# Casting and splitting the next weights ahead of, instead of behind, the background tasks of their slot

## The chip, the cores and the metric

The kernel runs on one core of a Trainium2 chip. The metric is the time of one execution on the device in microseconds (us), as the median of several runs; a profile of one further execution comes with it.

## What is computed

The reference passes one sequence of 256 tokens of width 2048 through three blocks, in float32. Cut to the products and what hangs on them:

```python
# block 1
proj = rms_norm(x) @ w_in                      # 2048 x 12288, split in ten
y_r  = rwkv7(p_r, p_k, p_v, ...) * silu(z_r)   # a recurrence over 256 tokens, 16 heads of 64
y_a  = band_attention(q, k, v) * silu(z_a)
merged = sigmoid(m_r) * (y_r @ w_branch_rwkv) + sigmoid(m_a) * (y_a @ w_branch_attn)
x = x + rms_norm(merged @ w_out)
# block 2
proj = rms_norm(x) @ w_in_2                    # queries, keys, index scores, gates
attn = top-k sparse attention;  sgu = spatial gating unit
x = x + (sigmoid(ga) * attn + sigmoid(gb) * sgu) @ w_out_2
x = x + relu(rms_norm(x) @ w_ff1) ** 2 @ w_ff2        # 2048 x 8192 x 2048
# block 3
x = rms_norm(x);  y = [pool_mixer, dilated attention] of rms_norm(x) @ w_in_3
x = x + [rms_norm(y_pool), rms_norm(y_attn)] @ w_out_3
x = x + relu(rms_norm(x) @ w_up) ** 2 @ w_down
out = rms_norm(x)
```

Most of the work is in some 580 MB of weights, each of which is read once and multiplied by 256 columns of activations.

## The kernel before

**Panels and groups.** Every weight matrix is cut into panels of 512 output columns (`Panel`, two are narrower). A panel's rows are taken in groups: one group is 512 rows by 512 columns, loaded as two halves (weight units) of 128 x 1024 floats, 512 KB each. A panel of a 2048-row matrix has four groups, one of a 1024-row matrix (the two branch matrices and the output matrix of block 3) has two. `Builder.run` (L187) walks over all groups of all panels in order. In a group it works through four output tiles, j = 0 to 3 (the code calls them units; I call one with what is issued after it a **slot**, and a weight unit always a half). Slot j issues 8 matmuls for each pair, 4 rows of tiles times 2: L250 multiplies the rounded weights `whi` by a 512-wide operand, which holds the rounded activations and their remainder, and L251 the weights' remainder `wlo` by the 256 rounded activations. All add up in the PSUM tile `pm` of tag m0 to m3; each tag has one buffer, so the next panel's tile j can be begun when this panel's has been read out. Panels in mode "T" swap the operands (L256 to L258) and have two slots.

**Weight units.** `cut(i, u)` (L202 to L213) makes half u of group i ready: ScalarE casts it (L210, `whi`), VectorE subtracts (L211, `wlo`). `whi` and `wlo` have four buffers each, which is two groups: the cast of half 0 of group i+1 can begin when the last matmuls of group i-1 that read half 0 are done, which is in that group's slot 3. While group i is multiplied, `cut(i + 1, 0)` is issued in slot 0 and `cut(i + 1, 1)` in slot 1. In mode T half 0 is cut ahead of the slots, and half 1 in slot 0.

**Evacuations.** When the last group of a panel has issued tile j, the panel's evacuation is started (`start`, L180, called in L261). Most begin with `sum_halves` (L270): ScalarE copies the right half of `pm` to `ev` (L273; L617, L697 and L1111 are the same copy in other panels), and a step later VectorE adds the left half (L276). So the copy waits for TensorE to finish that very tile. What follows differs by panel: gates, products, and the split of a result into `mg`, `hid` or `yah` (L281 on ScalarE, L283 on VectorE), which are operands of later panels.

**Background tasks.** Attention, the RWKV recurrence (`rwkv`, L729; its inner part `gram`, L917), top-k, the pooling mixer and the norms are Python generators. Each issues a few instructions on TensorE, VectorE, ScalarE, GpSimd or a DMA, then yields n, and is taken up again n steps later. They have no queue of their own: their instructions stand in the same in-order engine queues as the weights' and the matmuls'. The numbers of the yields are set by hand, so that a result is there by the time TensorE comes to the instruction that reads it.

**The order in a slot.** `step` (L132) first moves the evacuations on by a piece each, then each background task. Ahead of the change, a slot ends so:

```python
                self.step(j in when)          # evacuations, then background tasks
                if last:
                    self.start(p.evac(j, out))
                if j in when:
                    cut(i + 1, when.index(j))
```

`when` is (0, 1) for four slots. `busy` (true in a slot with a cut) holds older evacuations back for that slot, and some tasks (the axpy steps of the recurrence, L867 to L874, and top-k) skip it.

Of the kernel before, what the change touches and what calls it, by code (L numbers as in the profile page):

```python
# [66 lines left out]
class Builder:  # L67
# [62 lines left out]
        self.bgs.append([gen, 0])  # L130

    def step(self, busy=False):  # L132

        self.busy = busy
        lazy = 0 if busy else 3
        for e in list(self.evq):
            if e[1] and not lazy:
                continue
            lazy -= e[1]
            e[1] = 1  # L140
            if next(e[0], True):
                self.evq.remove(e)
        for b in list(self.bgs):
            if b[1] > 0:
                b[1] -= 1
                continue
            try:
                n = next(b[0])
                b[1] = (n or 1) - 1
            except StopIteration:  # L150
                self.bgs.remove(b)
# [29 lines left out]
    def run(self, panels):  # L181
        groups = [(p, g) for p in panels for g in range(p.ngroups)]
        n = len(groups)
        raw, split = {}, {}
        loaded = [0]

        def load(upto):  # L187
            while loaded[0] < min(upto, 2 * n):
                u = loaded[0]
                p, g = groups[u // 2]  # L190
                t = self.stage.tile([128, p.half, p.ncols], F32, name="wf", tag="wf", bufs=5)
                raw[u] = t
                k = g * p.kg + (u % 2) * p.half
                if p.load:
                    p.load(t, k)
                else:
                    src = p.w[p.c0 // p.ncols, (p.k0 + k) // p.half]
                    self.nc.sync.dma_start(t, src.rearrange("p (k c) -> p k c", c=p.ncols))
                self.after.pop(u, lambda: None)()
                loaded[0] += 1  # L200

        def cut(i, u):  # L202
            if i >= n:
                return
            p, g = groups[i]
            hs, ls = split.setdefault(i, ([], []))
            t = raw.pop(2 * i + u)
            hi = self.stage.tile([128, p.half, p.ncols], F32R, name="whi", tag="whi", bufs=4)
            lo = self.stage.tile([128, p.half, p.ncols], F32R, name="wlo", tag="wlo", bufs=4)
            self.nc.scalar.copy(hi, t)  # L210
            self.nc.vector.tensor_tensor(lo, t, hi.bitcast(F32), op=ALU.subtract)  # L211
            hs.append(hi)
            ls.append(lo)  # L213

        load(5)
        cut(0, 0)
        cut(0, 1)
        ps = {}
        nt = 1
        mm = self.nc.tensor.matmul  # L220
        for i, (p, g) in enumerate(groups):
            if g == 0 and p.pre:
                p.pre()
            load(2 * i + 7)
            hs, ls = split.pop(i)
            if g == 0:
                nt = (nt + 1) % 2 if p.mode == "T" else 1
                ps = {}
            last = g == p.ngroups - 1
            if p.mode == "F":  # L230
                units = [(j, f"m{j}") for j in range(p.ncols // 128)]
            else:
                units = [(j, f"m{2 * nt + j}") for j in range(2)]

            when = (0, 1) if len(units) == 4 else (-1, 0 if len(units) == 2 else -1)
            for u in range(2):
                if when[u] < 0:
                    cut(i + 1, u)
            for j, tag in units:
                if g == 0:  # L240
                    ps[j] = self.pm.tile([128, 512], F32, name="pm", tag=tag)
                out = ps[j]
                for kk in range(p.kg):
                    hi, lo = hs[kk // p.half][:, kk % p.half, :], ls[kk // p.half][:, kk % p.half, :]
                    a = p.act(g * p.kg + kk)
                    st = g == 0 and kk == 0
                    en = last and kk == p.kg - 1
                    if p.mode == "F":
                        c = slice(j * 128, (j + 1) * 128)
                        mm(out, hi[:, c], a, start=st, stop=False, skip_group_check=True)  # L250
                        mm(out[:, 256:512], lo[:, c], a[:, 0:256], start=False, stop=en, skip_group_check=True)  # L251
                    else:
                        ah = a[:, j * 128:(j + 1) * 128]
                        al = a[:, 256 + j * 128:256 + (j + 1) * 128]
                        o = out[:, :p.ncols]
                        mm(o, ah, hi, start=st, stop=False, skip_group_check=True)  # L256
                        mm(o, ah, lo, start=False, stop=False, skip_group_check=True)  # L257
                        mm(o, al, hi, start=False, stop=en, skip_group_check=True)  # L258
                self.step(j in when)
                if last:  # L260
                    self.start(p.evac(j, out))  # L261
                if j in when:
                    cut(i + 1, when.index(j))
                if p.mode == "T":
                    self.step()
            if last and p.post:
                p.post()
# [1484 lines left out]
```

## Time and profile before

| | |
|---|---|
| median of 3 runs | 3312.41 us (3309.85 to 3313.7) |
| profiled execution, its time | 3309.79 us |
| its span | 3307.9 us |
| TensorE matmul busy | 3238.6 us (98% of the span) |
| VectorE busy | 2076.2 us (63%) |
| ScalarE busy | 1710.5 us (52%) |
| GpSimd busy | 560.0 us (17%) |
| moved by DMA | 589.88 MB, mean 178 GB/s |

Some 1.9 us lie between the span and the execution's own time. Busy shares are means over very different stages: from 1300 to 2300 us and from 2600 to 3280 us two feed-forward blocks run nearly alone, while the recurrence runs beside the projections from about 350 to 720 us, and three attentions and the other tasks elsewhere. A mean of 98% on TensorE leaves 69.3 us of the span in which no matmul is shown, and these lie in a few stages.

### The profile page before, as it was taken

What the parts mean: (1) busy time and instruction counts of PE and PEld (TensorE: products, weight loads), DVE (VectorE), ACT (ScalarE), POOL (GpSimd) and SP (SyncE); (2) the same over time, 40 slices, a digit from 0 to 9 for tenths busy, and PEclk for the clock granted to TensorE, in tenths of its full rate; (3) what the DMA queues carried; (4) which work ended last, traced back from release to release, by engine and by line L of the source; (5) the groups of instructions that cost most, each with busy time, mean ns of one, the idle gap of its engine ahead of it and who ended that gap; (6) DMA issues with size and microseconds to landing.
All of it is one profiled execution on the core that took longest, in us unless ns stands there. A gap on an engine that the chain in (4) does not pass through costs nothing.

```text
span 3307.9 us, 50068 instructions
## 1 busy us (share of the span) xinstructions
PE 3238.6 (98%) x19182; PEld 2797.5 (85%) x19182; DVE 2076.2 (63%) x3058; ACT 1710.5 (52%) x2868; POOL 560.0 (17%) x570
## 2 busy tenths in 40 slices
PE   8999999999999999999999999999999999999998
PEld 7887778888778888888888888888888888888887
DVE  5677677666567556676565555557757665555556
ACT  5555444455443654455545455555455655545454
POOL 2232031214310421243000000003215200000001
PEclk9999999999899999999999999999999999999999
DMA  6544545456445555656655565556555565566554
GB/s 206 185 160 159 152 124 172 151 161 203 152 149 187 177 166 177 198 181 191 192 191 185 187 198 189 186 191 195 175 172 166 185 191 188 187 198 189 183 189 147
DMA packets 175583, 589.88 MB, mean 178 GB/s; under 512 B 28784, under 2 KB 31984, under 8 KB 175344
## 3 DMA queue, kind: packets, MB, share of 16 engines
q1 hardware_dynamic: 174624, 585.47, 55.8%
q8 instruction: 150, 2.46, 0.3%
q10 hardware_dynamic: 720, 1.22, 0.1%
q14 instruction: 89, 0.73, 0.1%
HBM read 582.95 MB, written 3.67 MB: 177 GB/s over the span
## 4 chain that ended last, share of the span: by engine, by line
PE 86%; DVE 6%; issue 3%; ACT 3%; POOL 1%; DMA 0%; DVEq 0%; POOLq 0%; ACTq 0%
PE pm L250 51%; PE pm L251 26%; DVE wlo L211 3%; PE pm L256 2%; PE pm L258 2%; PE pm L257 2%; ACT whi L210 2%; PE psc L341 1%; DVE ev L276 0%; PE ppv L375 0%; PE ptr L368 0%; POOL ev L671 0%; PE pst L302 0%; PE ppl L1622 0%; DMA b<-bias 0%
## 5 line engine op out<-in xcount | busy, mean ns | idle before, releaser
L211 DVE TENSOR_TENSOR wlo<-wf,whi 128x1024 fp32r<-128x1024 f32 x1086 | 1351.5, 1268 | 1091.8 <-ACT whi L210 1081.9
L250 PE MATMUL pm<-h,whi 128*128 128x512 f32 x3872 | 1377.0, 398 | 11.1 <-ACT whi L210 7.8
L210 ACT CAST whi<-wf 128x1024 fp32r<-128x1024 f32 x1086 | 1106.2, 1050 | 463.8 <-PE pm L250 374.2
L251 PE MATMUL pm<-h,wlo 128*128 128x256 f32 x3872 | 1091.4, 282 | 16.1 <-DVE wlo L211 15.6
L250 PEld LDWEIGHTS pm<-h,whi 128*128 128x128 f32 x3872 | 729.6, 188 | 181.5 <-ACT whi L210 8.2
L251 PEld LDWEIGHTS pm<-h,wlo 128*128 128x128 f32 x3872 | 735.4, 190 | 24.9 <-DVE wlo L211 24.2
L250 PE MATMUL pm<-hid,whi 128*128 128x512 f32 x2048 | 711.2, 391 | 0.0
L251 PE MATMUL pm<-hid,wlo 128*128 128x256 f32 x2048 | 573.5, 280 | 0.0
L273 ACT COPY ev<-pm 128x256 f32<-128x256 f32 x491 | 180.7, 368 | 702.9 <-PE pm L251 687.1
L250 PEld LDWEIGHTS pm<-hid,whi 128*128 128x128 f32 x2048 | 383.1, 187 | 84.8
L250 PE MATMUL pm<-hb,whi 128*128 128x512 f32 x1168 | 419.3, 401 | 12.1 <-DVE hb L727 9.2
L251 PEld LDWEIGHTS pm<-hid,wlo 128*128 128x128 f32 x2048 | 387.1, 189 | 0.0
L1103 POOL TENSOR_TENSOR acc<-acc,sqa 128x256 f32<-128x256 f32 x104 | 117.1, 1131 | 1497.7 <-ACT sqa L1098 1474.1
L251 PE MATMUL pm<-hb,wlo 128*128 128x256 f32 x1168 | 329.6, 282 | 1.4 <-DVE wlo L211 1.1
L250 PEld LDWEIGHTS pm<-hb,whi 128*128 128x128 f32 x1168 | 220.9, 189 | 68.2 <-issue 9.5
L251 PEld LDWEIGHTS pm<-hb,wlo 128*128 128x128 f32 x1168 | 223.0, 191 | 4.1 <-DVE wlo L211 2.9
L276 DVE TENSOR_TENSOR ev<-pm,ev 128x256 f32<-128x256 f32 x491 | 199.1, 417 | 25.5 <-ACT ev L273 25.1
L250 PE MATMUL pm<-mg,whi 128*128 128x512 f32 x512 | 178.0, 391 | 0.0
L251 PE MATMUL pm<-mg,wlo 128*128 128x256 f32 x512 | 143.7, 281 | 0.9 <-DVE wlo L211 0.9
L250 PEld LDWEIGHTS pm<-mg,whi 128*128 128x128 f32 x512 | 95.8, 187 | 21.2 <-DVE ev L276 0.2
L251 PEld LDWEIGHTS pm<-mg,wlo 128*128 128x128 f32 x512 | 96.8, 189 | 1.9 <-DVE wlo L211 1.9
L256 PE MATMUL pm<-whi,hb 128*128 128x512 f32 x160 | 66.0, 412 | 0.0
(350 smaller groups left out, 3004.5 us busy)
## 6 DMA issues: line engine op xcount, KB each, us to landing
wf<-w_in SPq DMA_DIRECT2D x312, 512.0 KB, 4.0
wf<-w_ff SPq DMA_DIRECT2D x256, 512.0 KB, 4.4
wf<-w_sgu SPq DMA_DIRECT2D x128, 512.0 KB, 3.9
wf<-w_up SPq DMA_DIRECT2D x128, 512.0 KB, 4.3
wf<-w_down SPq DMA_DIRECT2D x128, 512.0 KB, 4.4
wf<-w_out SPq DMA_DIRECT2D x96, 512.0 KB, 4.3
wf<-w_branch_attn SPq DMA_DIRECT2D x16, 512.0 KB, 3.6
wf<-w_branch_rwkv SPq DMA_DIRECT2D x16, 512.0 KB, 4.3
```

Source lines behind the costliest of these rows:

```text
L210: self.nc.scalar.copy(hi, t)
L211: self.nc.vector.tensor_tensor(lo, t, hi.bitcast(F32), op=ALU.subtract)
L250: mm(out, hi[:, c], a, start=st, stop=False, skip_group_check=True)
L251: mm(out[:, 256:512], lo[:, c], a[:, 0:256], start=False, stop=en, skip_group_check=True)
L256: mm(o, ah, hi, start=st, stop=False, skip_group_check=True)
L257: mm(o, ah, lo, start=False, stop=False, skip_group_check=True)
L258: mm(o, al, hi, start=False, stop=en, skip_group_check=True)
L273: nc.scalar.copy(a, p[:, 256:512])
L276: nc.vector.tensor_tensor(b, p[:, 0:256], a, op=ALU.add)
L341: nc.tensor.matmul(p[:, a:2 * a + 128], qa[:, a:a + 128], ka[:, 0:a + 128], start=True, stop=True)
L1103: nc.gpsimd.tensor_tensor(accs[0], accs[0], s, op=ALU.add)
```

## The change

`step` is divided in two: `evacs`, which moves the evacuations, and `tasks`, which moves the background tasks. In a slot with a weight unit, the unit is now cut between the two, and so also ahead of the start of the slot's own evacuation.

```diff
     def step(self, busy=False):
+        self.evacs(busy)
+        self.tasks()
+
+    def evacs(self, busy=False):
 
         self.busy = busy
         lazy = 0 if busy else 3
@@ -140,6 +144,9 @@
             e[1] = 1
             if next(e[0], True):
                 self.evq.remove(e)
+
+    def tasks(self):
+
         for b in list(self.bgs):
             if b[1] > 0:
                 b[1] -= 1
@@ -256,11 +263,12 @@
                         mm(o, ah, hi, start=st, stop=False, skip_group_check=True)
                         mm(o, ah, lo, start=False, stop=False, skip_group_check=True)
                         mm(o, al, hi, start=False, stop=en, skip_group_check=True)
-                self.step(j in when)
+                self.evacs(j in when)
+                if j in when:
+                    cut(i + 1, when.index(j))
+                self.tasks()
                 if last:
                     self.start(p.evac(j, out))
-                if j in when:
-                    cut(i + 1, when.index(j))
                 if p.mode == "T":
                     self.step()
```

The set of instructions is the same on every engine, and with line numbers left out the order on TensorE, GpSimd and SyncE (which issues the loads) is too. On ScalarE 365 of the 1086 casts stand further ahead, on VectorE 104 of the 1086 subtractions; the lines of the changed file are 7 or 8 higher (cast L217, subtraction L218, `ev` copy L281).

The first place is ScalarE at the end of the last panel ahead of those of `w_branch_rwkv` and in the first of those (about 750 us): `ev<-pm` are the copies of slots 0, 1, ..., the casts between them make the next group ready, and `mg` are splits of the branch's result. Before:

```order
L273 COPY ev<-pm 128x256
L210 CAST whi<-wf 128x1024
L273 COPY ev<-pm 128x256
L210 CAST whi<-wf 128x1024
L281 CAST mg<-ev_7650 128x256
L273 COPY ev<-pm 128x256
```

Now:

```order
L217 CAST whi<-wf 128x1024
L281 COPY ev<-pm 128x256
L217 CAST whi<-wf 128x1024
L281 COPY ev<-pm 128x256
L289 CAST mg<-ev_7650 128x256
L281 COPY ev<-pm 128x256
```

Each cast stands ahead of the copy of its own slot instead of behind it. 267 of the 365 moved casts pass such a copy, 240 of them nothing else. VectorE's order at this place is the same as before.

The second place is VectorE in the recurrence (about 390 us, at the end of a panel): `S`, `P`, `gs` and `yc` are results of background tasks, `ev` are evacuations. Before:

```order
L1008 TENSOR_TENSOR S<-pY,DC 128x256
L211 TENSOR_TENSOR wlo<-wf,whi 128x1024
L276 TENSOR_TENSOR ev_3934<-pm,ev 128x256
L559 TENSOR_TENSOR ev_3934<-ev_3934,rb 128x256
L929 TENSOR_TENSOR P<-pgr,mask_90 128x512 x2
L1037 TENSOR_REDUCE gs<-pY 128x4
L1038 TENSOR_SCALAR gs<-gs 128x4
L1040 TENSOR_TENSOR yc<-pY,gs 128x256
L211 TENSOR_TENSOR wlo<-wf,whi 128x1024
```

Now:

```order
L218 TENSOR_TENSOR wlo<-wf,whi 128x1024
L1016 TENSOR_TENSOR S<-pY,DC 128x256
L284 TENSOR_TENSOR ev_3934<-pm,ev 128x256
L567 TENSOR_TENSOR ev_3934<-ev_3934,rb 128x256
L218 TENSOR_TENSOR wlo<-wf,whi 128x1024
L937 TENSOR_TENSOR P<-pgr,mask_90 128x512 x2
L1045 TENSOR_REDUCE gs<-pY 128x4
L1046 TENSOR_SCALAR gs<-gs 128x4
L1048 TENSOR_TENSOR yc<-pY,gs 128x256
```

The two subtractions stand ahead of `S` and of the five instructions from `P` to `yc`; the evacuation's place among the tasks is the same. 52 of the 104 moved subtractions lie between 200 and 720 us by their time in the trace of before.

## Rows read from the trace of the kernel before

**Rows 1.** The page: the span and the engines' busy time.

```profile
span 3307.9 us, 50068 instructions
...
PE 3238.6 (98%) x19182; PEld 2797.5 (85%) x19182; DVE 2076.2 (63%) x3058; ACT 1710.5 (52%) x2868; POOL 560.0 (17%) x570
```

**Rows 2.** Busy time by stretch: length, busy of PE PEld DVE ACT POOL, PEclk, DMA.

```profile
12.00:260.00 248.00, 243.79 (x1421) 205.12 (x1420) 156.06 (x231) 126.56 (x209) 68.04 (x66) 1.00 0.53 172
260.00:280.00 20.00, 16.45 (x81) 13.31 (x80) 11.45 (x32) 7.65 (x22) 5.50 (x5) 0.83 0.69 238
...
340.00:352.00 12.00, 9.32 (x42) 7.27 (x41) 11.67 (x20) 6.01 (x11) 4.65 (x4) 0.86 0.59 162
...
400.00:490.00 90.00, 81.81 (x644) 67.83 (x645) 63.40 (x116) 45.23 (x88) 29.71 (x34) 0.96 0.38 112
490.00:600.00 110.00, 104.89 (x684) 89.05 (x683) 79.37 (x132) 46.79 (x67) 20.60 (x20) 0.98 0.59 181
...
750.00:803.00 53.00, 49.26 (x267) 40.53 (x266) 34.78 (x49) 28.31 (x50) 30.21 (x32) 1.00 0.61 206
...
885.00:928.00 43.00, 32.23 (x136) 25.48 (x137) 32.70 (x41) 21.67 (x46) 28.66 (x31) 0.76 0.31 91
928.00:1300.00 372.00, 366.63 (x1973) 308.93 (x1972) 222.77 (x369) 192.41 (x331) 68.25 (x82) 1.00 0.55 173
1300.00:2300.00 1000.00, 1000.00 (x5762) 879.98 (x5761) 618.34 (x816) 530.60 (x866) 131.42 (x111) 1.00 0.60 190
2300.00:2600.00 300.00, 296.08 (x1638) 254.79 (x1637) 211.12 (x316) 158.21 (x282) 102.32 (x98) 1.00 0.55 176
```

**Rows 3.** Who TensorE waited for: us in total, times, longest us.

```profile
PE pm L251 <- DVE wlo L211: 21.6, 27, 3.1
...
PE pm L250 <- DVE ev L276: 6.9, 12, 1.2
PE pbo L822 <- DVE ku L816: 2.3, 1, 2.3
...
PE pW L969 <- ACT UV L951: 1.5, 1, 1.5
```

**Rows 4.** The same list for all engines: ScalarE's and VectorE's waits around the cuts.

```profile
DVE wlo L211 <- ACT whi L210: 1081.9, 435, 7.3
ACT ev L273 <- PE pm L251: 687.1, 192, 8.3
ACT whi L210 <- PE pm L250: 374.2, 131, 6.7
```

**Rows 5.** Timeline of ScalarE from 750.5 us: start, us, what, idle before and releaser.

```profile
751.01 0.37 ACT L273 COPY ev<-pm 128x256 f32<-128x256 f32 x1 [2.50 <-PE pm L251]
751.28 1.06 ACT L210 CAST whi<-wf 128x1024 fp32r<-128x1024 f32 x1
752.42 0.37 ACT L273 COPY ev<-pm 128x256 f32<-128x256 f32 x1
...
756.51 0.41 ACT L281 CAST mg<-ev 128x256 fp32r<-128x256 f32 x1 [2.76 <-POOL ev L672]
...
758.66 2.00 ACT L210 CAST whi<-wf 128x1024 fp32r<-128x1024 f32 x2
```

**Rows 6.** Timeline of VectorE, same stretch.

```profile
752.37 1.23 DVE L211 TENSOR_TENSOR wlo<-wf,whi 128x1024 fp32r<-128x1024 f32 x1 [3.22 <-ACT whi L210]
753.51 0.42 DVE L276 TENSOR_TENSOR ev<-pm,ev 128x256 f32<-128x256 f32 x1
...
759.74 3.28 DVE L211 TENSOR_TENSOR wlo<-wf,whi 128x1024 fp32r<-128x1024 f32 x2 [0.52 <-ACT whi L210]
```

**Rows 7.** Timeline of GpSimd, same stretch: the first and the last product on `ev`.

```profile
754.07 1.58 POOL L671 TENSOR_TENSOR ev<-ev,mr 128x256 f32<-128x256 f32 x1 [39.83 <-DVE ev L276]
...
760.35 1.60 POOL L672 TENSOR_TENSOR ev<-ev,ua 128x256 f32<-128x256 f32 x1
```

**Rows 8.** Timeline of GpSimd around 260 us: the attention's mask.

```profile
264.84 0.30 POOL L500 MEMSET b<- 64x256 f32 x1 [23.95 <-DMA b<-bias]
```

## The prediction

> **What bounds the kernel now.** The page comes first: TensorE shows matmuls for 3238.6 of 3307.9 us [rows 1]. Nothing else is near its limit, and the change takes no matmul away, so it can only win what TensorE loses. The busy time by stretch says where that is. From 1300 to 2300 us no time at all is lost [rows 2], and there the change can win nothing. The other stretches shown lose, as length less busy: 4.2 us from 12 to 260, 3.6 from 260 to 280, 2.7 from 340 to 352, 8.2 from 400 to 490, 5.1 from 490 to 600, 3.7 from 750 to 803, 10.8 from 885 to 928, 5.4 from 928 to 1300 and 3.9 from 2300 to 2600. The granted clock adds to it: where it is 0.86 over 12 us, 0.14 x 12 = 1.7 us of full speed are missing, after a stall in the same stretch; likewise 3.6 us from 400 to 490, 2.2 from 490 to 600, 3.4 from 260 to 280 and 10.3 from 885 to 928 [rows 2]. In all of these the clock is for a part of the stretch at the lower of its two levels, 1.2 GHz, and TensorE had waited there before.
>
> The list of waits says for what: 27 times for `wlo` (21.6 us), 12 times for an evacuation's sum (6.9 us), and for single results of tasks such as `ku` (2.3) and `UV` (1.5) [rows 3]. The waits of the other engines lead to the cause. VectorE is not short of time on the whole: it stood idle for 1081.9 us in front of a subtraction whose cast was not done, 435 times [rows 4]. And ScalarE stood for 687.1 us in front of an `ev` copy whose tile TensorE was still computing [rows 4]. A cast behind such a copy waits for that tile too, though it does not need it.
>
> The timeline at 751 us shows one such place. The copy of slot 0 waits 2.50 us for TensorE; the cast behind it begins at 751.28 [rows 5]. VectorE idles 3.22 us, subtracts from 752.37, and only then, at 753.51, adds the evacuation that ScalarE had copied at 751.38 [rows 6]. GpSimd, which waits for that sum, begins at 754.07 [rows 7]; ScalarE waits for GpSimd with the split `mg` at 756.51, and the next two casts come at 758.66 behind it [rows 5]. TensorE runs out of weights there: panels of this kind lose most of the 3.7 us from 750 to 803 [rows 2].
>
> **The change, part by part.** No instruction is added or removed, and nothing moves on TensorE, GpSimd or SyncE: no load is issued elsewhere, and GpSimd's own queue keeps its order.
>
> *Casts ahead of `ev` copies* (267 of the 365 moved casts). A cast takes 1.06 us, a slot 752.42 - 751.01 = 1.41 us [rows 5]. The buffer that the first cast needs comes free in slot 3 of the group before, and the copy cannot begin before TensorE has ended slot 0, so the cast fits ahead of the copy and delays it by nothing. It is done some 2 us earlier (slot 0 of 1.41 us and the end of the slot before it), the subtraction too (1.23 us [rows 6]), and VectorE then takes the sum at about 751.4 instead of 753.51. GpSimd starts 2 us sooner and the casts behind `mg` follow. Worth: the whole 3.7 us from 750 to 803. In the feed-forward stretches this move costs and wins nothing, since TensorE already waits for nothing there.
>
> *Units ahead of tasks where VectorE is full.* From 340 to 352 us VectorE is busy for 11.67 of 12 us [rows 2]: the late subtractions stand behind the splits of task results and behind idle time that arose at the panel's end just before. 2.7 us of waiting and 1.7 of clock are at stake; I take 4.0.
>
> *The recurrence and its neighbours* (400 to 490 and 490 to 600) lose 8.2 + 3.6 and 5.1 + 2.2 us, the output panels of block 3 (2300 to 2600) 3.9 us. The first bound is nothing, if another instruction is late at once; the other is all 23.0. I take two thirds, 15.3: the waits on `wlo` and on `ev` go, and those on task results only in part. From 928 to 1300 us (top-k, attention, mixing) I take half of 5.4, or 2.7. From 12 to 260 us 2.3 of the 4.2 are the one wait for `ku` [rows 3], which stays; of the rest 1.4. From 260 to 280 us the first loss is a mask that the tasks load and that lands late (GpSimd waits 23.95 us for it [rows 8]); no order of the cuts helps, so 0.5. From 885 to 928 us TensorE waits for a norm's results, which go step by step over three engines; four such steps and two units stand in each group in either order, and the change only swaps neighbours. I take 1.0.
>
> Sum of the gains: 3.7 + 4.0 + 15.3 + 2.7 + 1.4 + 0.5 + 1.0 = 28.6 us, between nothing and 47.7 (36.8 of idle and 10.9 of clock in these stretches, without 885 to 928).
>
> *What is given back.* A task's result in slot 0 or 1 now waits for a cast and a subtraction. For ScalarE that is 1.06 us, for VectorE 1.23 us and whatever the cast is late. A slot of 1.41 us hides one subtraction, so a result that TensorE reads a slot later still arrives; what suffers is a result that is read in the slot in which it is made. In `gram` the copies `UV` are such: four times in the kernel (c = 0 and 2 in each half), each late by up to one subtraction, 4 x 1.2 = 5 us. For `ku`, which is already awaited, I add 1.2. Bounds: nothing, and one subtraction and its wait on all 52 moved subtractions of 200 to 720 us, which is the second rival. I take 6.
>
> Net: 28.6 - 6 = 23 us. Against the profiled execution's own 3309.8 us that gives 3287; the median of the runs is 2.6 us above it, so **3289 us**.
>
> *A rule that speaks against it.* A subtraction takes 1.23 us at 752.37, and two take 3.28 us together at 759.74, 1.64 each, while GpSimd multiplies [rows 6, 7]; GpSimd's product takes 1.60 us beside it. The subtraction reads two tiles of SBUF. The Trainium skill, "SBUF — State Buffer", section "Who interferes with whom", says that a VectorE instruction with two SBUF inputs contends with a GpSimd instruction that reads SBUF, that whichever comes first holds the read interface for its whole length, and that the other one blocks. The rows agree in that both get longer, though by 0.4 us and not by the other's whole length. By that rule, units that now fall on GpSimd's busy time, which itself moves, would cost more; it is the third rival.
>
> **The rivals.**
>
> *No change.* The wait only moves to another instruction: VectorE has as much to do as before, and where it is full (11.67 of 12 us [rows 2]) some reader is late in any order. Against it: the 1081.9 us in which VectorE was idle ahead of subtractions [rows 4], and the idle 3.22 us [rows 6] just ahead of a stall. Time: 3310 to 3312. Chance 0.13.
>
> *Slower: task results late.* The tasks' distances in slots were set by hand to the order as it was. VectorE now stops at a subtraction whose cast waits for a buffer, with tasks' results behind it that could have been made, and TensorE, in its own fixed order, stands at their readers in the recurrence. The price is up to one subtraction, 1.23 us, of waiting for each of the 52 moved ones: from 0.55 us each on (28.6 / 52) the gain is gone. At 0.85 each, 44 us are paid, and the time is 3312 + 44 - 29 = 3327. For it: TensorE already waits for `ku` and `UV` [rows 3], so these have no slack. Against it: these are 3.8 us in all, and most results have two or three slots. Chance 0.10.
>
> *Port.* If each of the 27 waits for `wlo` [rows 3] keeps 0.4 us of contention that the earlier start had to win back, 11 us less are gained: 23 - 11 = 12, or 3300. Chance 0.05.
>
> *All of it.* The waits go without any new one: 47.7 us, 3264. Chance 0.10.
>
> **How the numbers follow.** The forecast has 0.62, and by its own bounds reaches from 3275 to 3302. A difference of under 0.2%, 6.6 us, can't be told from none. Forecast, port and "all of it" lie beyond that on the fast side: 0.77. "No change" is the same: 0.13; slower 0.10. The range from 3266 to 3310 leaves out the slower rival, half of "no change" and about half of "all of it": 0.2.
>
> **What would show it.** Right: from 750 to 803 us TensorE is busy for over 52.5 us; the cast at that panel's end begins ahead of the `ev` copy; ScalarE's 687 us in front of `ev` copies shrink and its 374.2 us of casts waiting for TensorE [rows 4], that is for a buffer, grow by most of it; TensorE's waits for `wlo` and `ev` fall from 28.5 us to under 10; the clock falls in fewer places between 340 and 600 us; from 1300 to 2300 us nothing changes. Wrong: new waits of TensorE for `UV`, `P`, `ws` or `ku` that together pass 20 us, or waits for `wlo` of the old size.

## The result, and the profile after

The changed kernel takes 3268.27 us in the median of 4 runs (3265.34 to 3268.97); beside it the kernel before took 3312.06 us (3309.85 to 3313.7). The ratio is 0.9868, with a 95% interval from 0.9855 to 0.988: 43.8 us are gained where 23 were forecast. The direction held, and the range by 2.3 us at its fast end (3266); the size forecast is about half of what came.

The page of the changed kernel, against [rows 1]: the span is 41.0 us shorter, and TensorE shows 18.1 us less for the same 19182 matmuls.

```profile
span 3266.9 us, 49936 instructions
...
PE 3220.5 (99%) x19182; PEld 2792.2 (85%) x19182; DVE 2105.7 (64%) x3058; ACT 1729.9 (53%) x2868; POOL 535.7 (16%) x570
```

The next view is busy time by stretch in the changed kernel. TensorE's order is the same in both kernels, so each stretch here is bounded by the starts of the very matmuls that stand at the bounds of one in [rows 2]: the first answers to 12 to 260 us, then 260 to 280, 340 to 352, 400 to 490, 490 to 600, 750 to 803, 885 to 928, 1300 to 2300 and 2300 to 2600. What a stretch gained is the difference of the two lengths. Columns as in [rows 2].

```profile
11.92:261.29 249.37, 245.35 (x1420) 206.89 (x1420) 161.36 (x235) 130.05 (x213) 68.09 (x66) 0.99 0.56 177
261.29:274.77 13.48, 13.48 (x81) 11.26 (x80) 12.75 (x34) 7.64 (x22) 5.39 (x5) 1.00 0.70 246
334.26:343.06 8.80, 7.65 (x43) 6.22 (x42) 8.77 (x13) 4.36 (x8) 3.73 (x3) 1.00 0.53 142
390.36:476.91 86.55, 80.91 (x646) 66.46 (x644) 60.97 (x107) 43.70 (x85) 28.95 (x34) 0.98 0.36 110
476.91:580.15 103.24, 101.89 (x683) 87.82 (x682) 83.05 (x135) 48.95 (x68) 20.09 (x20) 1.00 0.61 190
728.66:775.64 46.98, 46.98 (x268) 40.61 (x266) 35.87 (x49) 27.39 (x49) 30.33 (x32) 1.00 0.66 219
858.55:900.96 42.41, 31.85 (x137) 24.75 (x137) 34.15 (x44) 22.36 (x46) 29.61 (x31) 0.80 0.30 87
...
1269.20:2267.17 997.97, 997.97 (x5762) 879.90 (x5761) 623.99 (x814) 537.33 (x865) 116.08 (x110) 1.00 0.60 190
2267.17:2559.71 292.54, 292.35 (x1638) 254.59 (x1637) 211.01 (x317) 160.65 (x283) 94.55 (x98) 1.00 0.58 180
```

In two stretches that lost time before, TensorE is now busy throughout: 13.48 us instead of 20.00, and 46.98 instead of 53.00. The last one, 292.54 us instead of 300.00, still shows 0.2 us without a matmul. The first stretch of the program became 1.4 us longer.

Who TensorE waited for, against [rows 3]: `wlo` from 21.6 us in 27 waits to 3.7 in 7, `ev` from 6.9 to 1.9, but `ku` from 2.3 to 4.2.

```profile
PE pbo L830 <- DVE ku L824: 4.2, 2, 3.6
PE pm L258 <- DVE wlo L218: 3.7, 7, 0.7
PE pW L977 <- DVE UV L957: 2.4, 3, 1.1
...
PE pm L257 <- DVE ev L284: 1.9, 2, 1.0
```

The same list for ScalarE and VectorE, against [rows 4]. ScalarE stands less in front of the copy (687.1 us before) and more in front of the cast, which waits for its buffer (374.2 before). VectorE's idle time ahead of subtractions (1081.9 before) fell by 143 us.

```profile
DVE wlo L218 <- ACT whi L217: 938.7, 550, 7.5
ACT whi L217 <- PE pm L257: 786.6, 294, 6.1
ACT ev L281 <- PE pm L258: 309.9, 310, 4.9
```

The panel end of [rows 5 to 7] again, first ScalarE. The cast at 727.37 has gone ahead of the copy at 729.57, and the copy still begins when TensorE lets it.

```profile
727.37 1.05 ACT L217 CAST whi<-wf 128x1024 fp32r<-128x1024 f32 x1 [1.80 <-issue]
729.57 0.37 ACT L281 COPY ev<-pm 128x256 f32<-128x256 f32 x1 [1.15 <-PE pm L258]
...
735.07 2.00 ACT L217 CAST whi<-wf 128x1024 fp32r<-128x1024 f32 x2
```

VectorE at that place: the sum follows its copy at once (729.97), where it came 2.1 us behind it (753.51 against 751.38).

```profile
728.46 1.23 DVE L218 TENSOR_TENSOR wlo<-wf,whi 128x1024 fp32r<-128x1024 f32 x1 [2.25 <-ACT whi L217]
729.97 0.42 DVE L284 TENSOR_TENSOR ev<-pm,ev 128x256 f32<-128x256 f32 x1 [0.29 <-ACT ev L281]
```

From the copy of slot 0 to the two casts behind `mg` it takes 735.07 - 729.57 = 5.5 us, where it took 758.66 - 751.01 = 7.65 [rows 5].

### The profile page after: what moved, and what is told of

Its sections match the earlier page's. It is cut to its first block, busy times and chain, and to the rows that moved or that the text cites. A ratio compares the mean times of both kernels' runs of the same rounds, so it can differ in the third digit from the quotient of the medians.

```text
span 3266.9 us, 49936 instructions
## 1 busy us (share of the span) xinstructions
PE 3220.5 (99%) x19182; PEld 2792.2 (85%) x19182; DVE 2105.7 (64%) x3058; ACT 1729.9 (53%) x2868; POOL 535.7 (16%) x570
## 4 chain that ended last, share of the span: by engine, by line
PE 81%; DVE 3%; issue 2%; ACT 1%; POOL 1%; DVEq 0%; POOLq 0%; ACTq 0%
PE pm L257 48%; PE pm L258 25%; PE pm L263 2%; PE pm L265 2%; PE pm L264 2%; DVE wlo L218 1%; ACT whi L217 0%; PE psc L349 0%; PE ppv L383 0%; POOL x L730 0%; PE ptr L376 0%; PE ppl L1630 0%; PE pmx L1436 0%; POOL acc L1111 0%; DVE mr L1383 0%
## 5 line engine op out<-in xcount | busy, mean ns | idle before, releaser
L218 DVE TENSOR_TENSOR wlo<-wf,whi 128x1024 fp32r<-128x1024 f32 x1086 | 1337.8, 1258 | 945.0 <-ACT whi L217 938.7
L217 ACT CAST whi<-wf 128x1024 fp32r<-128x1024 f32 x1086 | 1106.7, 1050 | 936.0 <-PE pm L257 786.6
L281 ACT COPY ev<-pm 128x256 f32<-128x256 f32 x491 | 182.4, 372 | 320.8 <-PE pm L258 309.9
L284 DVE TENSOR_TENSOR ev<-pm,ev 128x256 f32<-128x256 f32 x491 | 206.2, 421 | 117.7 <-ACT ev L281 117.0
```

What stands on the lines that cost most here:

```text
L281: nc.scalar.copy(a, p[:, 256:512])
L284: nc.vector.tensor_tensor(b, p[:, 0:256], a, op=ALU.add)
```

## The experiments

Two theories were set against each other. **A**: the gain comes from ScalarE, whose casts no longer stand behind a copy of a tile that is still being computed. **B**: it comes from VectorE, whose subtractions no longer stand behind the splits of task results. **C** concerns the mask at 260 us alone. The third edit is made on the kernel before, the others on the changed kernel or on the kernel with the cast alone, as said there. In the order of issue that kernel has evacuations, unit, tasks, start of the own evacuation.

**The unit ahead of the slot's own evacuation only.**

```diff
                 self.evacs(j in when)
+                self.tasks()
                 if j in when:
                     cut(i + 1, when.index(j))
-                self.tasks()
                 if last:
                     self.start(p.evac(j, out))
```

> The unit stands ahead of its slot's own evacuation (which matters in a panel's last group alone), but behind the tasks again; 267 of the 365 moved casts keep their move. Theory A (the gain comes from casts that no longer stand behind a copy of a tile that TensorE is still computing): the gains at 260 to 280 us (6.7 us), 750 to 803 (6.1) and 2300 to 2600 (7.8) stay whole, those at 340 to 352 (3) and half of those at 400 to 600 (10) go; TensorE waits for no UV and for ku as before; 3272 to 3280 us. Theory B (the gain comes from VectorE, whose subtractions no longer stand behind the splits of task results): little over a third of the 43.8 us stays, 3294 us or more.

Measured: 3270.35 us, ratio 0.9876 (0.9862 to 0.9889). 41.7 of the 43.8 us are there. In its trace VectorE's order is that of the kernel before, instruction for instruction; what moved is 276 casts on ScalarE, 267 of them past an `ev` copy and 9 past other readers of a fresh `pm` tile. So these 41.7 us are ScalarE's order alone, and B falls. A's figures were too careful: from 400 to 600 us the same matmuls take 9.9 us less than before, where half of some 10 had been expected; only 340 to 352 us lost most of its gain (1.2 left of 3.2). The gain in the recurrence comes from panel ends too.

**The unit ahead of the tasks, but with the old order in a panel's last group.**

```diff
                 self.evacs(j in when)
-                if j in when:
+                if j in when and not last:
                     cut(i + 1, when.index(j))
                 self.tasks()
                 if last:
                     self.start(p.evac(j, out))
+                if j in when and last:
+                    cut(i + 1, when.index(j))
```

> The unit stands ahead of the tasks in every group but a panel's last, where the old order is kept. Theory A: only the 340 to 352 us stretch and part of 400 to 600 us gain, and the later ku and UV cost their 3 to 5 us: 3300 to 3308 us, with the mask's stall at 268 us and the stalls for weights and evacuations at 750 to 803 us as before. Theory B: most of the gain is here, 3285 us or less. If the two parts add up, the gains of this kernel and of the one ahead of the copy alone make 43.8 us together.

Measured: 3311.05 us, ratio 0.9996 (0.9987 to 1.0005): no difference that can be told, less than A expected. Here 89 casts and 75 subtractions stand further ahead, and two effects that are told apart below can cancel. The two parts add up: 41.7 + 1.0 = 42.7, against 43.8 for both.

**One cast.** On the kernel before; `ncut` counts the units, and 77 is the second half of the group at 249 us. The edit passes a single cast ahead of a single instruction, `vt`, which reads a `pm` tile as a copy does; on every other engine the order stays. The lines that count `ncut` are left out here.

```diff
                 self.step(j in when)
+                first = j in when and self.ncut == 77
+                if first:
+                    cut(i + 1, when.index(j))
                 if last:
                     self.start(p.evac(j, out))
-                if j in when:
+                if j in when and not first:
                     cut(i + 1, when.index(j))
```

> The kernel before with a single cast moved: the second one ahead of the group at 249 us goes ahead of one evacuation copy, vt. Theory C: the mask lands late because its load stands in SyncE's queue behind the write of LT, LT on VectorE behind this cast's subtraction, the cast on ScalarE behind vt, and vt waits for TensorE. Then LT comes some 3 us earlier, the mask too, and the 3.08 us wait for wlo at 268 us goes, with the low clock behind it: 5 to 7 us gained, 3305 to 3307 us. Rival: the mask is early in the changed kernel because the loads of many earlier weights are ahead; then one cast gains under 1 us: 3311 to 3312 us.

Measured: 3304.88 us, ratio 0.9978 (0.9969 to 0.9986): 7.2 us from one moved instruction. The whole chain of theory C can be read. In the kernel before, ScalarE:

```profile
249.16 0.69 ACT L490 ACTIVATE vt<-pm,rt 128x512 f32<-128x512 f32 x1 [4.33 <-PE pm L258]
249.75 1.04 ACT L210 CAST whi<-wf 128x1024 fp32r<-128x1024 f32 x1
```

VectorE there, with `LT` ready to be made but behind the subtraction:

```profile
250.82 1.23 DVE L211 TENSOR_TENSOR wlo<-wf,whi 128x1024 fp32r<-128x1024 f32 x1 [4.73 <-ACT whi L210]
251.96 0.68 DVE L848 TENSOR_TENSOR LT<-pLT,mask 128x512 f32<-128x512 f32 x1
```

SyncE's queue there, in which the mask's load stands behind the write of `LT`:

```profile
252.67 1.94 SPq L855 DMA_DIRECT2D d<-LT  x4
...
258.04 0.38 SPq L499 DMA_DIRECT2D b<-bias  x1
```

With the one cast moved, ScalarE, VectorE, SyncE's queue and GpSimd, which waits for the mask:

```profile
244.60 1.04 ACT L212 CAST whi<-wf 128x1024 fp32r<-128x1024 f32 x1 [0.30 <-PE pm L260]
248.63 0.69 ACT L495 ACTIVATE vt<-pm,rt 128x512 f32<-128x512 f32 x1 [2.98 <-PE pm L260]
```

```profile
246.82 0.69 DVE L853 TENSOR_TENSOR LT<-pLT,mask 128x512 f32<-128x512 f32 x1
```

```profile
247.54 1.94 SPq L860 DMA_DIRECT2D d<-LT  x4
...
252.91 0.38 SPq L504 DMA_DIRECT2D b<-bias  x1
```

```profile
259.11 0.30 POOL L505 MEMSET b<- 64x256 f32 x1 [18.77 <-DMA b<-bias]
```

`LT`, its write and the mask's load are each 5.1 us earlier (0.5 of it is from ahead of 250 us) and the mask 5.7 (264.84 before [rows 8]). The matmuls of 262 to 280 us take 6.7 us less: TensorE's wait for `wlo` of 3.08 us at 268.56 us is gone, and from 262 to 275 us it is busy throughout at a granted clock of 1.00. The rival (under 1 us) falls.

**The cast alone.** `cut` is divided into `cast` (ScalarE) and `subtract` (VectorE); the casts keep their new places, the subtractions have their old ones.

```diff
                 self.evacs(j in when)
                 if j in when:
-                    cut(i + 1, when.index(j))
+                    cast(i + 1, when.index(j))
                 self.tasks()
                 if last:
                     self.start(p.evac(j, out))
+                if j in when:
+                    subtract(i + 1, when.index(j))
```

> The changed kernel with the casts in their new places, but every subtraction in its old one, behind the tasks and the slot's own evacuation. Theory A (ScalarE's order is what counts): all of the gain stays except at 340 to 352 us, and the waits for UV (2.4 us) and the longer one for ku (4.2 against 2.3 us), with the low clock behind them, are not paid: 3263 to 3270 us. Theory B (VectorE's order counts): 3290 us or more, with waits for wlo near their old 21.6 us.

Measured: 3259.53 us, ratio 0.984 (0.9827 to 0.9853): 52.5 us faster than the kernel before, and by 8.7 us faster than the changed kernel, whose interval (0.9855 to 0.988) does not touch this one. No other kernel here is faster. B falls again, since VectorE's order is that of the kernel before here too. A held, with more gained than its range said, and even where it had made an exception, for 340 to 352 us take 8.70 us instead of 12.00. ScalarE's order is that of the changed kernel, so the 8.7 us are what the changed kernel's 104 moved subtractions cost. Who TensorE waited for: `ku` and `UV` have shrunk, `wlo` has grown by less than they gave back.

```profile
PE pm L268 <- DVE wlo L225: 6.9, 9, 2.5
...
PE pbo L842 <- DVE ku L836: 1.4, 1, 1.4
...
PE pW L989 <- ACT UV L971: 0.5, 1, 0.5
```

One of the places is the copy `UV` of `gram`. In the changed kernel it stands on VectorE behind a subtraction,

```profile
411.45 1.23 DVE L218 TENSOR_TENSOR wlo<-wf,whi 128x1024 fp32r<-128x1024 f32 x1 [0.52 <-ACT whi L217]
412.71 0.42 DVE L957 COPY UV<-pvt 64x256 f32<-64x256 f32 x1
```

and TensorE waits for it, after which 411 to 418 us have a granted clock of 0.76:

```profile
413.18 0.37 PE L977 MATMUL pW<-UV,P 64*64 64x64 f32 x1 [1.13 <-DVE UV L957]
```

With the cast alone the two copies come first and the two subtractions behind them:

```profile
407.60 0.42 DVE L969 COPY UV<-pvt 64x256 f32<-64x256 f32 x1 [0.78 <-ACT UV L971]
...
409.43 2.35 DVE L225 TENSOR_TENSOR wlo<-wf,whi 128x1024 fp32r<-128x1024 f32 x2
```

**The cast alone, but behind the tasks.** In the kernel above, `self.tasks()` goes ahead of `cast`.

> The kernel with the cast alone moved, but the cast stands behind the tasks again and ahead of the slot's own evacuation only; subtractions stay in their old place. It lies between two measured kernels: the whole unit ahead of the copy, behind the tasks (3270.35 us), and the cast alone ahead of tasks and copy (3259.53 us). Theory D (the 11 us between them are paid by subtractions that stand ahead of other work on VectorE): 3259 to 3263 us, TensorE's waits for wlo under 9 us. Theory E (they come from casts that no longer stand behind the tasks' instructions on ScalarE): 3267 to 3271 us, and waits for wlo near 11 us.

Measured: 3271.13 us, ratio 0.9876 (0.9862 to 0.9889). On every engine the order in this trace is that of the first experiment, so it is that kernel once more (3270.35 us there), and it says nothing about where a subtraction should stand. From the kernel with the cast alone it differs by 120 casts on ScalarE, with VectorE's order the same. So theory D falls for this pair and E holds, with 10.8 us of waits for `wlo`: casts behind the tasks' instructions cost 11.6 us. That a subtraction ahead of the *tasks* costs too is shown by the changed kernel against the cast alone. The largest single place: these two rows of the busy time by stretch are the same 72 or 73 matmuls, first with the cast behind the tasks,

```profile
465.00:480.00 15.00, 13.18 (x72) 10.84 (x72) 11.46 (x16) 5.10 (x6) 5.95 (x7) 0.89 0.53 148
```

then with the cast ahead of them:

```profile
463.03:474.22 11.19, 11.19 (x73) 9.54 (x73) 10.26 (x14) 4.20 (x5) 5.02 (x6) 1.00 0.58 181
```

ScalarE shows why, in the slower one: it waits 3.10 us for VectorE in front of a task's copy `pv`, and behind that stand three casts which need nothing of it. The faster kernel has the same wait (3.11 us), but there one of these three, begun at 459.31 us, stands ahead of it.

```profile
467.18 0.26 ACT L1084 COPY pv<-pyt 64x128 f32<-64x128 f32 x1 [3.10 <-DVE pv L1082]
467.34 2.94 ACT L215 CAST whi<-wf 128x1024 fp32r<-128x1024 f32 x3
```

TensorE, in the slower one, waits for the first of the three and then for its subtraction; in the faster one it waits for nothing in this stretch. These 1.8 us of waiting and the clock (0.11 x 15 = 1.7 us) make 3.5 of the 3.8 us.

```profile
468.44 0.49 PE L267 MATMUL pm<-h,whi 128*128 128x512 f32 x1 [0.69 <-ACT whi L215]
...
470.06 0.44 PE L268 MATMUL pm<-h,wlo 128*128 128x256 f32 x1 [1.13 <-DVE wlo L225]
```

**The whole unit ahead of the later stages of evacuations too.** In the changed kernel, `cut` goes ahead of `self.evacs`.

> The changed kernel with the whole unit, cast and subtraction, ahead of the later stages of earlier evacuations too. Theory D (on VectorE a subtraction costs those behind it up to its 1.23 us and the wait for its cast): the sums of ev stand behind it, TensorE's waits for ev grow from 1.9 to 10 us or more, and the sums that GpSimd and ScalarE's splits wait for come later; 3280 to 3300 us. Rival (the earlier the unit, the better): 3262 to 3268 us.

Measured: 3296.6 us, ratio 0.9949 (0.9936 to 0.9961); TensorE waits for `ev` 18.4 us in 14 waits (1.9 in 2 in the changed kernel). Against that kernel 266 subtractions and only 5 casts stand further ahead, and it takes 28.3 us more. As theory D said: on VectorE, what TensorE or GpSimd is waiting for must not stand behind a subtraction. Earlier is not better.

**The cast ahead of those stages, the subtraction in its old place.** In the kernel with the cast alone, `cast` goes ahead of `self.evacs`.

> The kernel with the cast alone moved (3259.53 us), with the cast ahead of the later stages of earlier evacuations as well; subtractions stay in their old place. Theory A (what counts is only that a cast does not stand behind a copy of an unfinished tile): those later stages are ready when they are issued, so it makes no difference of more than 4 us: 3256 to 3264 us. Rival (the cast waits for its weight buffer, and ready splits now stand behind it): waits for ev, ua or P of TensorE grow and it takes 3270 us or more.

Measured: 3260.86 us, ratio 0.9843 (0.9829 to 0.9856). No difference that can be told, as A said; but this edit puts only 5 casts ahead of anything, so it hardly tests A or its rival.

**Each subtraction a slot later.** In the kernel with the cast alone, `subtract` is issued in slots 1 and 2 instead of 0 and 1.

```diff
-                if j in when:
-                    subtract(i + 1, when.index(j))
+                if j > 0 and j - 1 in when:
+                    subtract(i + 1, when.index(j - 1))
```

> The kernel with the cast alone moved, with each subtraction one slot (1.41 us) later still. Theory D at its end: task results and sums on VectorE are earlier by up to 1.23 us each and the weights still in time, 3254 to 3260 us. Rival (the subtraction is then late for TensorE, and its buffer late for the next load): waits for wlo grow from 6.9 to 15 us or more, 3268 to 3290 us.

Measured: 3295.15 us, ratio 0.9946 (0.9934 to 0.9958); TensorE waits 28.5 us in 34 waits for `wlo`. On VectorE 511 subtractions stand further back, on ScalarE nothing moves. The rival holds, and more strongly than it said. So of the four places tried the subtraction's best is between: behind the tasks of its own slot, not behind those of the next.

## Why the direction was right and the size too small

By stretch, in us. Predicted are the terms of the sum (two thirds of each loss in three of them; what was to be given back is put where it was expected). The last column is the kernel with the cast alone. The bounds of its stretches are found as above.

| stretch before | predicted | changed kernel | cast alone |
|---|---|---|---|
| 12 to 260 | 1.4 - 1.2 | -1.4 | 2.3 |
| 260 to 280 | 0.5 | 6.5 | 6.7 |
| 340 to 352 | 4.0 | 3.2 | 3.3 |
| 400 to 490 | 7.9 - 5 | 3.5 | 6.1 |
| 490 to 600 | 4.9 | 6.8 | 6.7 |
| 750 to 803 | 3.7 | 6.0 | 6.1 |
| 885 to 928 | 1.0 | 0.6 | 2.2 |
| 928 to 1300 | 2.7 | 3.8 | 4.5 |
| 1300 to 2300 | 0 | 2.0 | 2.0 |
| 2300 to 2600 | 2.6 | 7.5 | 6.6 |
| elsewhere | 0 | 2.6 | 4.5 |

How far such figures can be trusted shows in the one-cast kernel, whose order behind 250 us is that of before: from 280 us on its stretches differ from before by 0.7 us at most, but 928 to 1300 takes 2.1 us longer and 1300 to 2300 1.7 us.

**Right: the mechanism at a panel's end.** The cast goes ahead of the copy and does not delay it, the sum and what follows come some 2 us earlier, ScalarE's time in front of `ev` copies went where it was said to go, and the stalls at 750 to 803 us vanish. The first experiment has 41.7 us from this alone. By name the prediction gave these casts 3.7 of its 28.6 us; for the rest it names stages and does not say which of the moves earns it. Of the signs that were named, TensorE's waits for `wlo` and `ev` (28.5 us, now 5.6) and the 412 us by which casts wait longer for their buffers came as said; "from 1300 to 2300 us nothing changes" did not: five kernels with the casts ahead of the copies take 998.0 us there, where before has 1000.1 and the one-cast kernel, with the order of before, 1001.7.

**Wrong: "no order of the cuts helps"** at 260 to 280 us (0.5 us). It measured 6.5, and the one-cast experiment shows the reason. The late mask was read as a cause, because GpSimd waits for a DMA there [rows 8]. But a DMA has a place in a queue: its issue stood behind the write of `LT`, and so on back to a cast behind `vt`. The prediction stopped at the landing and did not ask what SyncE's queue had waited for.

**Mis-sized: the price of a stall.** Each loss was taken as length less busy time [rows 2]. But the bars of matmuls overlap in this profile, and the overlap hides part of every stall. The kernel before at a place with two of them:

```profile
2567.49 0.28 PE L251 MATMUL pm<-ah,wlo 128*128 128x256 f32 x1
2567.61 0.39 PE L250 MATMUL pm<-ah,whi 128*128 128x512 f32 x1
2568.06 0.39 PE L251 MATMUL pm<-ah,wlo 128*128 128x256 f32 x1
2568.28 0.39 PE L250 MATMUL pm<-ah,whi 128*128 128x512 f32 x1
2568.51 0.28 PE L251 MATMUL pm<-ah,wlo 128*128 128x256 f32 x1
2569.28 0.50 PE L250 MATMUL pm<-ah,whi 128*128 128x512 f32 x1 [0.48 <-DVE ev L276]
```

From a `wlo` product to the next `whi` product it is 2567.61 - 2567.49 = 0.12 us undisturbed, from a `whi` to a `wlo` 2568.51 - 2568.28 = 0.23. The wait at 2569.28 shows 0.48 us of idle time, but the start comes 0.77 - 0.12 = 0.65 us late; and at 2568.06 a start is 0.45 - 0.23 = 0.22 us late with no idle time shown at all. So some 0.17 us are missing from this wait, and the other is missing altogether. Of the waits with idle time in the kernel before, 48 show none in the changed kernel (places of low clock apart): by starts they are worth 27.5 us, by idle time 19.8, which is 0.16 us more for each. In the whole trace idle time fell by 69.3 - 46.4 = 22.9 us; the clock, by length times what it lacks of 1.00 in the stretches shown, gave 21.2 - 12.7 = 8.5 (both clocks are rounded, so this is rough); the other 10 or so of the 41.0 are in the main what bars had hidden. That is why 750 to 803 us gave 6.0 where 3.7 were thought to be all. Of the 2.0 us from 1300 to 2300 only 0.6 lie in six late starts; the rest are steps of 0.01 us between matmuls, and what causes these is open.

**Mis-sized: two thirds** of 490 to 600 and 2300 to 2600 us. The third held back was for task results that would be late at once. In the first of the two TensorE waits for none, in the second for one, 0.2 us. From 400 to 490 us the net term (2.9) is near the 3.5 measured: TensorE waits 5.0 us for task results and `ua` there, 2.0 of them for `UV`.

**Right in kind, too low: what is given back.** It was put at 6 us. The kernel with the cast alone shows it by its difference to the changed kernel, 8.7 us. `UV` and `ku` are as foreseen among those that pay: TensorE waits 3.3 us for `UV` in the changed kernel and 0.5 with the cast alone; the wait for `ku` grew by 1.9 us in all, not 1.2, and low clock came with it.

**Wrong engine: 340 to 352 us.** The prediction had late subtractions behind splits on a full VectorE. With subtractions in their old order the stretch gains as much (3.3 us), and with casts behind the tasks 1.2. It is the cast here too. More generally the change was taken as one piece. Its half on ScalarE gains and its half on VectorE costs; the prediction even named both, as gain and as give-back, without seeing that they can be had apart.

**Luck in the range.** Its fast end stood for waits that all go. The time came near that end for other reasons: 6.5 us from a place where no order was to help, and some 10 that the sum did not count.

**The rivals.** "No change" and "task results late" did not come, though the mechanism of the second is what the 8.7 us are. "All of it" was nearest in time (3264), but not in kind: by the measured terms there was more to win than its 47.7 us, and new waits did come. "Port" would show in longer subtractions. Their mean is 1258 ns against 1268 before:

```profile
L218 DVE TENSOR_TENSOR wlo<-wf,whi 128x1024 fp32r<-128x1024 f32 x1086 | 1337.8, 1258 | 945.0 <-ACT whi L217 938.7
```

What the prediction read from [rows 6, 7], that both instructions get longer by 0.4 us and not by the other's whole length, does not hold one by one. In the kernel before, VectorE and then GpSimd:

```profile
759.74 1.61 DVE L211 TENSOR_TENSOR wlo<-wf,whi 128x1024 fp32r<-128x1024 f32 x1 [0.52 <-ACT whi L210]
...
761.28 1.75 DVE L211 TENSOR_TENSOR wlo<-wf,whi 128x1024 fp32r<-128x1024 f32 x1
```

```profile
759.52 0.75 POOL L671 TENSOR_TENSOR ev<-ev,mr 128x256 f32<-128x256 f32 x1
760.35 1.60 POOL L672 TENSOR_TENSOR ev<-ev,ua 128x256 f32<-128x256 f32 x1
```

The product at 759.52 came first and keeps its 0.75 us. Each of the next three begins while the other engine's is still running: the subtraction at 759.74 (1.61 us instead of 1.23), the product at 760.35 (1.60 instead of 0.75), the subtraction at 761.28 (1.75). They are longer by 0.38, 0.85 and 0.52 us, where 0.53, 1.00 and 0.67 us of the other one were left, each time 0.15 less. So at this place the second one waits for what is left of the first, and this agrees with the rule of the Trainium skill, "SBUF — State Buffer", section "Who interferes with whom", that the other one blocks. The changed kernel has the same lengths there. The cost that "Port" forecast did not come, as the mean shows.

## What to carry to other kernels

An instruction that is ready should not stand in an in-order queue behind one that waits for something it doesn't need; but this is to be asked for each engine apart, since the same step earlier on ScalarE gained 52.5 us with the subtraction left where it was, and the subtraction's move cost 8.7 of them. A late DMA is followed back through the queue that issues it to what stood ahead of it there. And a stall is priced by the starts of the instructions beside it, not by the idle time that the profile leaves between bars.

## What the runs showed that had not been expected

At the same `ku` read, a wait of 2.3 us in the kernel before left the granted clock of 220 to 245 us at 1.00, and a wait of 3.6 us in the changed kernel was followed by the lower of the two levels (1.2 GHz): 231 to 236 us have 0.66, that is 0.34 x 5 = 1.7 us more. So 1.3 us of waiting cost about 3. The length of the wait alone does not decide it: in the kernel before a wait of 1.45 us for `UV` at 423.42 us was followed by the lower level too (425 to 429 us have 0.57). How the two waits differ in what TensorE had done ahead of them was not tried.

What remains open: of the 11.6 us that casts behind the tasks cost, one place of 3.8 us was read; the others were not traced to single instructions.
